# Scaling and shifting the transposed tokens in one VectorE step, with the modulation's last products reordered, in a one-core backbone layer

## The chip, the cores and the metric

The kernel runs on one NeuronCore of one Trainium2 chip. A time is the device time of one execution in microseconds. The trace is that of one profiled execution of the kernel before; its span runs from the first to the last instruction.

## The reference

One layer: a token-mixing block (windowed attention beside an mLSTM) and a SwiGLU block, each between norms, for 1024 latent tokens and 256 context tokens of width 1024, all in float32. What the change touches is the entrance of the layer, and one place where the mixing block's output projection meets the next norm:

```python
mod_x = (silu_c @ w_ada[layer] + b_ada[layer])[:, None, :]
mod_c = silu_cc @ w_ada[layer] + b_ada[layer]
sh_m, sc_m, gt_m, sh_f, sc_f, gt_f = jnp.split(mod_x, 6, axis=-1)
...
px = modulate(rms_norm(x, g_pre_mix[layer]), sh_m, sc_m) @ w_in[layer]
pc = modulate(rms_norm(ctx, g_pre_mix[layer]), csh_m, csc_m) @ w_in[layer]
...
mix_x = jnp.concatenate([att_x, ml_x], axis=-1) @ w_out[layer]
x = x + gt_m * rms_norm(mix_x, g_post_mix[layer])
```

with `modulate(h, shift, scale) = h * (1 + scale) + shift`.

## The kernel before

Every product that matters is taken in parts: `split` writes a value's rounded high half with a ScalarE cast and the rest, its low half, with a VectorE subtraction (L61, L62). `mm3` (L73 to L75) then issues three matmuls: high by high, high by low, low by high, on TensorE (PE in the profile).

**Modulation (L283 to L361).** For the sections scale (`sec` 1) and then shift (`sec` 0), eight 512 KB blocks `wa` of the weights arrive by DMA one after another. Five of a section's blocks are split into scratch space in `hh` and `hl`, and PE takes one pair of matmuls with the high half and one with the low half; three blocks (the table `PLAIN`) go through PE as plain float32. The sums `pr` have 4 rows; they are copied to SBUF (the first half by ScalarE, L344, the second by VectorE, L345), transposed into `pcol`, and combined into the per-channel columns `scol` (scale) and `hcol` (shift, L361). In section 0 the split of block 3 takes its low half on GpSimd (L302), and block 3's and block 6's low products are issued late. The first weights `w1` of the layer are split meanwhile, by `w1_split` (L274, L279).

**Token preparation (L184 to L256).** There are ten tiles of 128 tokens, 0 to 7 latent and 8 and 9 context. For each: load and sum of squares (`prep_a`, L190), scaling of the tokens (`xt`, L197, on GpSimd for most), eight transposes on PE into two PSUM halves `pt` (`prep_t`, L209), then per half a multiplication by `scol` on VectorE (`prep_m`, L223), an addition of `hcol` (`prep_b`, L236; on VectorE for tiles 0 and 1, on GpSimd from tile 2 on), a cast to `hh` (ScalarE, L251; for the first half of tile 0 L248 does all from PSUM) and the low half `hl` (VectorE, L252). `pt` has two buffers (tag `tp`) for tiles 1 to 9, so that a half can be transposed only when the half two before it has been read.

**First projections (L364 to L454).** `s1(i)` multiplies tile i by `w1`: 24 matmuls of 128x272 in two groups of 12, the first needing the first halves of `hh` and `hl`, the second the second halves (for tile 0 all `hh` products come first, L381, then the `hl` products, L384). Its sums go to the gate table `G` (VectorE, L398 and L400), to `av` (ScalarE L61 and VectorE L62) and to `V` (ScalarE, L403). `s2(i)` does the same with the second weights `w2`, whose halves are made by L450 and L451 in the turns of tiles 1 and 2; three tiles of `s2` are put between the `s1` from turn 3 on.

**What sets the order here.** From the start of the kernel to the end of these projections the order on each engine is chosen by a scheduler that works with its own table of costs; `tc.keep_in_program_order` pins single instructions to the written order. Each engine then works through its queue strictly in that order.

**Output projection (L1304 to L1336).** Here the written order holds (`tc.manual_schedule`). In turn n, `omm` multiplies row tile n, `opost1` and `opost2` form the norm, the residual and the next norm of tile n-1 (squares L1183 and L1191, scaling L1193), `otr` transposes its result on PE (L1205), `omod` modulates it (L1214), and `mixsplit(n, hf)` (L1170) splits one half of the mixing output of tile n into `mh` and `ml` for `omm`.

Of the kernel before, what the change touches and what calls it, by code (L numbers as in the profile page):

```python
# [9 lines left out]
F32 = mybir.dt.float32  # L10
F32R = mybir.dt.float32r
AF = mybir.ActivationFunctionType
# [4 lines left out]
P = 128  # L17
# [23 lines left out]
def body(tc, x, ctx, vecs, bcv, bada, gqm, gqf, wada, ws1, ws2, wt, wout, wfi, wfo,  # L41
# [156 lines left out]

    pts = {}

    def prep_t(i, keep=False):

        xt = xts.pop(i)
        pts[i] = []
        for b in range(2):
            pt = pa.tile([P, 4, P], F32, name="pt", tag="tp" if i else "mm", bufs=2 if i else 4)
            for k in range(4):
                kk = 4 * b + k
                t = pe.transpose(pt[:, k, :], xt[:, kk * P:(kk + 1) * P], ident)  # L209
                if keep and not kk:  # L210
                    tc.keep_in_program_order(t)
            pts[i].append(pt)

    raw2 = {}

    def prep_m(i):

        if i not in pts:
            prep_t(i)
        rw = hraw.pop(i)  # L220
        raw2[i] = [rw[:, 4 * b:4 * b + 4] for b in range(2)]
        for b in range(2):
            r = dve.tensor_tensor(raw2[i][b], pts[i][b], hcast(scol[:, i // NT, 4 * b:4 * b + 4]), MUL)  # L223
            if i == 1:
                tc.keep_in_program_order(r)

    def prep_b(i):

        if i not in raw2:
            prep_m(i)  # L230
# [3 lines left out]
        raws_ = raw2.pop(i)  # L234
        for b in (1, 0) if i == 0 else range(2):
            r = (dve if i < 2 else pool).tensor_tensor(raws_[b], raws_[b], hcast(hcol[:, q, 4 * b:4 * b + 4]), ADD)  # L236
            if i < 2:
                tc.keep_in_program_order(r)
            if i == 0 and b:
                w1_split(1, (1,))  # L240
        if i == 0:
            r2 = st[:, 12:13]
            tc.keep_in_program_order(dve.reciprocal(r2, r2))
        for b in range(2):
            h_ = hs[b][:, :, tok]
            if i + b == 0:
                for k in range(4):
                    act.activation(h_[:, k], pts[i][b][:, k], AF.Identity, scale=scol[:, q, k:k + 1],  # L248
                                   bias=hcol[:, q, k:k + 1])
            else:  # L250
                tc.keep_in_program_order(act.copy(h_, raws_[b]))  # L251
            r = dve.tensor_tensor(ls[b][:, :, tok], raws_[b], h_.bitcast(F32), SUB)  # L252
            if i == 0:
                tc.keep_in_program_order(r)
        if i == 0:
            prep_a2(2)  # L256
# [26 lines left out]
    PLAIN = {1: (0, 2, 4), 0: (0, 2, 7)}  # L283
    last, nsp, late = None, 0, []

    wm = pa.tile([P, 4, P], F32, name="warm", tag="tp", bufs=2)
    for i in range(11):
        pe.matmul(wm[:, i % 4], ones, ones, start=True, stop=True)
    for sec in (1, 0):
        pr = [pa.tile([4, 512], F32, name=f"pr{sec}{i}", tag="mm", bufs=4) for i in range(2)]  # L290
        for kt in range(KT):
            w = R(8 + kt, f"wa{sec}_{kt}", (D,))
            with tc.issue_after(last) if last is not None else ExitStack():
                last = dma(w, wada[kt * P:(kt + 1) * P, sec * D:(sec + 1) * D]).ins
            if kt in PLAIN[sec]:
                ops = ((cz4, w),)
            else:
                wh, wl = (t[1 - nsp // 4 % 2][:, nsp % 4] for t in (hh, hl))
                nsp += 1
                if (sec, kt) == (0, 3):  # L300
                    act.copy(wh, w)
                    pool.tensor_tensor(wl, w, wh.bitcast(F32), SUB)  # L302
# [5 lines left out]
            if (sec, kt) == (0, 3):  # L308
                low3 = ops.pop()
            if (sec, kt) == (0, 4):  # L310
                ops.insert(1, low3)
            if (sec, kt) == (0, KT - 2):
                late = ops[1:]
                ops = ops[:1]
            if (sec, kt) == (0, KT - 1):
                ops += late
            for n, (k, a, b) in enumerate(ops):
                for i in range(2):
                    r = pe.matmul(pr[i], a[:, k, :], b[:, i * 512:(i + 1) * 512], start=kt == 0 and n == 0,
                                  stop=kt == KT - 1 and n == len(ops) - 1)  # L320
                    if late:
                        tc.keep_in_program_order(r)
            if (sec, kt) == (0, 1):
                for i in range(2):
                    with tc.issue_after(last):
                        prep_a(i)
                        last = xd[i].ins
            if (sec, kt) == (0, 2):
                prep_t(0, True)
            if (sec, kt) == (0, 7):  # L330
                for i in range(2):
                    with tc.issue_after(last):
# [11 lines left out]
        act.copy(r4[:, 0:512], pr[0])  # L344
# [1619 lines left out]
```

## Time and profile before

| what | value |
|---|---|
| three runs | 1199.36, 1200.81, 1200.82 us; median 1200.81 us |
| profiled execution, its own time | 1200.47 us |
| its span | 1198.7 us (1.8 us lie around it) |
| PE busy | 1177.0 us, 98% of the span |
| VectorE (DVE) busy | 816.3 us |
| ScalarE (ACT) busy | 575.0 us |
| GpSimd (POOL) busy | 155.7 us |
| PE idle in the span | 21.7 us |

In the profile L12 is line 12 of the kernel before. Times of a timeline row are its start and its duration in us; a bracket behind a row is the idle time of its engine just before it and what ended that. The view of stretches gives, for each stretch, its length, the busy time (and the number of instructions) of PE, PE's weight loads, DVE, ACT and POOL, then the clock granted to PE as a share of full speed, the DMA share and GB/s. Rows of matmuls overlap: one starts before the modelled end of the one ahead.

### The profile page before, as it was taken

The numbers are of one execution on the slowest core, as the hardware profiler recorded it, in microseconds if no ns is written. First come the engines' busy times: TensorE is split into PE (matmuls) and PEld (weight loads), VectorE is DVE, ScalarE is ACT, GpSimd is POOL, SyncE is SP. The second block draws the span as 40 slices with busy tenths as digits, with TensorE's granted clock in tenths as the row PEclk, the third lists the DMA queues.
The fourth block names the chain that finished last, engine by engine and source line by source line (L and its number), as shares of the span: only waits on it lengthen the run. The fifth ranks groups of instructions, "written<-read, shape, count | busy, mean of one in ns | idle before, by whom it ended". The sixth has DMA issues, their size and how long they took to land.

```text
span 1198.7 us, 16356 instructions
## 1 busy us (share of the span) xinstructions
PE 1177.0 (98%) x5881; PEld 967.4 (81%) x5881; DVE 816.3 (68%) x1435; ACT 575.0 (48%) x1067; POOL 155.7 (13%) x197
## 2 busy tenths in 40 slices
PE   8899999999999999999999999999999999999997
PEld 3799888877878788788788888888888888888886
DVE  5863768853888795458877678676777656544567
ACT  5743442222777795687534333333333335434443
POOL 1550001215444461000000000000000000000000
PEclk9999999999999999999999999999999999999999
DMA  9522955557679971421133565656554557665853
GB/s 364 194 71 60 370 194 172 180 156 227 176 217 240 315 234 53 178 87 71 62 123 132 202 220 206 208 218 237 202 167 124 201 176 259 203 215 187 304 189 127
DMA packets 104616, 225.37 MB, mean 188 GB/s; under 512 B 10068, under 2 KB 39380, under 8 KB 103128
## 3 DMA queue, kind: packets, MB, share of 16 engines
q1 hardware_dynamic: 104536, 224.34, 56.3%
q8 instruction: 46, 0.75, 0.3%
q14 instruction: 34, 0.28, 0.1%
HBM read 162.43 MB, written 61.21 MB: 187 GB/s over the span
## 4 chain that ended last, share of the span: by engine, by line
PE 68%; DVE 4%; ACT 2%; issue 1%; DMA 0%; SPq 0%; POOL 0%; DVEq 0%; ACTq 0%
PE xv L75 8%; PE xv L73 8%; PE xv L74 8%; PE pt L75 6%; PE pt L74 6%; PE pt L73 6%; PE op L75 2%; PE op L73 2%; PE op L74 2%; PE fx L73 2%; PE fx L75 2%; PE fx L74 2%; PE pt L871 1%; PE pt L867 1%; PE pt L985 1%; PE fy L73 1%
## 5 line engine op out<-in xcount | busy, mean ns | idle before, releaser
L62 DVE TENSOR_TENSOR fo<-fr,fo 128x1024 fp32r<-128x1024 f32 x77 | 92.7, 1222 | 71.1 <-ACT fo L61 69.6
L61 ACT CAST fo<-fr 128x1024 fp32r<-128x1024 f32 x77 | 79.6, 1051 | 74.0 <-PE pt L75 36.5
L598 PE MATMUL t<-hh,th 128*128 128x512 f32 x208 | 82.4, 396 | 0.0
L599 PE MATMUL t<-hl,th 128*128 128x512 f32 x208 | 81.7, 393 | 0.0
L1380 ACT CAST wS<-wr 128x512 fp32r<-128x512 f32 x88 | 54.2, 622 | 56.1 <-PE pt L75 37.4
L1382 DVE TENSOR_TENSOR wS<-wr,wS 128x512 fp32r<-128x512 f32 x88 | 60.4, 689 | 20.7 <-ACT wS L1380 20.7
L73 PE MATMUL xv<-tT,wS 128*128 128x512 f32 x168 | 66.0, 393 | 0.0
L601 PE MATMUL t<-hh,tl 128*128 128x512 f32 x208 | 65.9, 394 | 0.0
L75 PE MATMUL xv<-tT,wS 128*128 128x512 f32 x168 | 65.6, 391 | 0.0
L74 PE MATMUL xv<-tT,wS 128*128 128x512 f32 x168 | 65.5, 390 | 0.0
L75 PE MATMUL op<-woh,ml 128*128 128x512 f32 x128 | 50.1, 392 | 1.5 <-DVE ml L62 1.5
L73 PE MATMUL op<-woh,mh 128*128 128x512 f32 x128 | 51.0, 398 | 0.0
L74 PE MATMUL op<-wol,mh 128*128 128x512 f32 x128 | 50.0, 390 | 0.0
L1131 DVE TENSOR_TENSOR wr<-wr 128x512 f32<-128x512 f32 x66 | 45.5, 690 | 1.4
L1414 ACT ACTIVATE es<-es 128x512 f32<-128x512 f32 x22 | 13.9, 632 | 66.5 <-DVE es L1134 66.5
L598 PEld LDWEIGHTS t<-hh,th 128*128 128x128 f32 x208 | 39.1, 188 | 8.2 <-issue 0.3
L599 PEld LDWEIGHTS t<-hl,th 128*128 128x128 f32 x208 | 39.1, 188 | 7.7 <-issue 0.7
L601 PEld LDWEIGHTS t<-hh,tl 128*128 128x128 f32 x208 | 37.4, 188 | 7.6 <-issue 1.4
L955 PE MATMUL s<-k,qh 128*128 128x256 f32 (+1 forms) x128 | 41.1, 331 | 2.0 <-ACT so L775 0.9
L73 PE MATMUL pt<-fo 128*128 128x512 f32 x110 | 42.8, 389 | 0.0
L75 PE MATMUL pt<-fo 128*128 128x512 f32 x110 | 42.8, 389 | 0.0
L74 PE MATMUL pt<-fo 128*128 128x512 f32 x110 | 42.8, 389 | 0.0
(1006 smaller groups left out, 3408.7 us busy)
## 6 DMA issues: line engine op xcount, KB each, us to landing
wr<-in_wfi SPq DMA_DIRECT2D x44, 512.0 KB, 4.6
wb<-in_wada SPq DMA_DIRECT2D x24, 512.0 KB, 6.0
s_d<-a SPq DMA_DIRECT2D x22, 512.0 KB, 6.9
bt<-in_wfo SPq DMA_DIRECT2D x44, 256.0 KB, 3.8
tb_d<-bt SPq DMA_DIRECT2D x11, 1024.0 KB, 3.9
fr<-s_d SPq DMA_DIRECT2D x44, 256.0 KB, 4.4
fr<-tb_d SPq DMA_DIRECT2D x44, 256.0 KB, 4.3
fr<-a_d SPq DMA_DIRECT2D x33, 256.0 KB, 4.5
```

What stands on the lines that cost most here:

```text
L61: act.copy(hi, raw)
L62: dve.tensor_tensor(lo, raw, hi.bitcast(F32), SUB)
L73: pe.matmul(ps, a[0], b[0], start=first, stop=False, **kw)
L74: pe.matmul(ps, a[0], b[1], start=False, stop=False, **kw)
L75: pe.matmul(ps, a[1], b[0], start=False, stop=last, **kw)
L598: pe.matmul(o, wh[:, kt], m[0], start=f, stop=False)
L599: pe.matmul(o, wh[:, kt], m[1], start=False, stop=False)
L601: pe.matmul(o, wl[:, kt], m[0], start=False, stop=l)
L955: pe.matmul(o, qh[:, h, :], k2[g][:, kc], start=True, stop=False)
L1131: dve.tensor_tensor(out, a, b, SUB)
L1380: act.copy(w[:, 0], raw)
L1382: dve.tensor_tensor(w[:, 1], raw, w[:, 0].bitcast(F32), SUB)
```

## The change

Four edits, of which three concern the first 80 us.

1. *Scaling and shifting in one step.* `prep_m` is gone. `prep_raw` reads each `pt` half from PSUM in four VectorE instructions of 128x128, each multiplying by one column of `scol` and adding one column of `hcol` (L219 of the new kernel, `tensor_scalar` with two per-partition operands). It stands in for one multiplication and one addition of 128x512. GpSimd keeps only the scaling of `xt`. Because the step needs `hcol`, nothing of it runs ahead of the shift columns any more; before, the multiplications of tiles 0 and 1 did.
2. *The modulation's last products.* Block 3 of section 0 is split like the others, its low half on VectorE. The products of blocks 3 to 7 are collected and issued in a fixed order: high 3, high 4, low 3, high 5, low 4, [first half of tile 1's transposes], high 6, low 5, plain 7, low 6, [second half of those transposes]. The copy of the first half of `pr` is pinned behind the casts of `w1`.
3. *Buffers.* The warm-up tile moves from tag `tp` to tag `mm`.
4. *Output projection.* In turn 2 alone, `mixsplit(2, 0)` is written ahead of `opost1(1)` instead of behind it.

```diff
-                if keep and not kk:
+                if keep:
                     tc.keep_in_program_order(t)
...
-        for b in range(2):
-            r = dve.tensor_tensor(raw2[i][b], pts[i][b], hcast(scol[:, i // NT, 4 * b:4 * b + 4]), MUL)
-            if i == 1:
-                tc.keep_in_program_order(r)
...
+    def prep_raw(i, b):
+
+        q = i // NT
+        raw = hraw[i][:, 4 * b:4 * b + 4]
+        for k in range(4):
+            kk = 4 * b + k
+            r = dve.tensor_scalar(raw[:, k], pts[i, b][:, k], scol[:, q, kk:kk + 1], hcol[:, q, kk:kk + 1], MUL, ADD)
+            if i < 2:
+                tc.keep_in_program_order(r)
+        return raw
...
-        for b in (1, 0) if i == 0 else range(2):
-            r = (dve if i < 2 else pool).tensor_tensor(raws_[b], raws_[b], hcast(hcol[:, q, 4 * b:4 * b + 4]), ADD)
...
+            if b not in raws_:
+                raws_[b] = prep_raw(i, b)
...
-    wm = pa.tile([P, 4, P], F32, name="warm", tag="tp", bufs=2)
+    wm = pa.tile([P, 4, P], F32, name="warm", tag="mm", bufs=4)
...
-                if (sec, kt) == (0, 3):
-                    act.copy(wh, w)
-                    pool.tensor_tensor(wl, w, wh.bitcast(F32), SUB)
-                else:
-                    split(wh, wl, w)
+                split(wh, wl, w)
...
+            if (sec, kt) > (0, 2) and not sec:
+                late += ops
+                ops = ()
             if (sec, kt) == (0, KT - 1):
-                ops += late
+
+                ops = late = [late[k] for k in (0, 2, 1, 4, 3, 6, 5, 8, 7)]
             for n, (k, a, b) in enumerate(ops):
+                if late and n == 5:
+                    prep_t(1, True, (0,))
...
-            if (sec, kt) == (0, 6):
-                prep_t(1, True)
-                prep_m(0)
-                prep_m(1)
+        if sec == 0:
+            prep_t(1, True, (1,))
...
-        act.copy(r4[:, 0:512], pr[0])
+        r = act.copy(r4[:, 0:512], pr[0])
+        if sec == 0:
+            tc.keep_in_program_order(r)
...
+        if n == 2:
+            mixsplit(n, 0)
         opost1(n - 1)
-        mixsplit(n, 0)
+        if n != 2:
+            mixsplit(n, 0)
```

On VectorE, just behind the low halves of tile 0, the kernel before had these rows (`hraw_234` is tile 1, `hraw_319` tile 2; `hh_101`, `hl_103` are first halves, `hh_102`, `hl_104` second halves):

```order
L236 TENSOR_TENSOR hraw_234<-hraw_234,hcol 128x512 x2
L398 TENSOR_TENSOR G<-slab,bcr 128x2x4
L400 TENSOR_TENSOR G<-slab,bcr 128x2x4
L223 TENSOR_TENSOR hraw_319<-pt,scol 128x512
L252 TENSOR_TENSOR hl_103<-hraw_234,hh_101 128x4x128
L223 TENSOR_TENSOR hraw_319<-pt,scol 128x512
L252 TENSOR_TENSOR hl_104<-hraw_234,hh_102 128x4x128
L62 TENSOR_TENSOR av_91<-slab,av_91 128x128
L435 RECIPROCAL st<-st 128x1
L252 TENSOR_TENSOR hl_103<-hraw_319,hh_101 128x4x128
```

In the new kernel the same place on VectorE reads so (`hraw_234` is tile 1, `hraw_315` tile 2):

```order
L219 TENSOR_SCALAR hraw_234<-pt,scol,hcol 128x128 x4
L247 TENSOR_TENSOR hl_103<-hraw_234,hh_101 128x4x128
L219 TENSOR_SCALAR hraw_234<-pt,scol,hcol 128x128 x4
L387 TENSOR_TENSOR G<-slab,bcr 128x2x4
L389 TENSOR_TENSOR G<-slab,bcr 128x2x4
L219 TENSOR_SCALAR hraw_315<-pt,scol,hcol 128x128 x5
L247 TENSOR_TENSOR hl_104<-hraw_234,hh_102 128x4x128
L219 TENSOR_SCALAR hraw_315<-pt,scol,hcol 128x128 x3
L62 TENSOR_TENSOR av_91<-slab,av_91 128x128
```

Tile 1's second low half now stands behind five of the eight steps of tile 2, and the remaining three stand ahead of `av`.

Further on, on VectorE behind the preparation of tile 2, the kernel before had (`w2l_477` is the low half of the second weights, `hraw_366` tile 4; tile 3's multiplications were ahead of this place):

```order
L451 TENSOR_TENSOR w2l_477<-wr_0_478,w2h_476 128x768
L398 TENSOR_TENSOR G<-slab,bcr 128x2x4
L400 TENSOR_TENSOR G<-slab,bcr 128x2x4
L223 TENSOR_TENSOR hraw_366<-pt,scol 128x512
L451 TENSOR_TENSOR w2l_477<-wr_2_482,w2h_476 128x768
```

The new kernel has there (`w2l_493` the same weights, `hraw_368` tile 3):

```order
L440 TENSOR_TENSOR w2l_493<-wr_0_494,w2h_492 128x768
L387 TENSOR_TENSOR G<-slab,bcr 128x2x4
L389 TENSOR_TENSOR G<-slab,bcr 128x2x4
L440 TENSOR_TENSOR w2l_493<-wr_2_498,w2h_492 128x768
L219 TENSOR_SCALAR hraw_368<-pt,scol,hcol 128x128 x8
```

All eight steps of tile 3 stand behind both weight rows and behind the gate rows of tile 2; on PE, tile 3's transposes stand behind all of `s1(2)`, and tile 4's first half directly behind them.

In the output projection, ScalarE had in turn 2 (`t_5211` is tile 1's norm, `mh` the half of tile 2 in question):

```order
L1214 ACTIVATE mix<-pt,hfc,sfc 128x128 x8
L1183 ACTIVATE t_5211,st<-op 128x1024
L178 ACTIVATE st<-st,epst 128x1
L61 CAST mh<-mix 128x512
L61 CAST b11h<-mix 128x4x128
L1191 ACTIVATE t_5211,st<-xt_5113 128x1024
```

and has now (`t_5255` is tile 1's norm):

```order
L1203 ACTIVATE mix<-pt,hfc,sfc 128x128 x8
L61 CAST mh<-mix 128x512
L1172 ACTIVATE t_5255,st<-op 128x1024
L178 ACTIVATE st<-st,epst 128x1
L61 CAST b11h<-mix 128x4x128
L1180 ACTIVATE t_5255,st<-xt_5153 128x1024
```

The cast of `mh` moved from behind the first square of tile 1's norm to ahead of it.

More of the change, by code (lines that the diff above doesn't have):

```diff
@@ L199, in body, with prep_t @@
     pts = {}
-    def prep_t(i, keep=False):
-        xt = xts.pop(i)
-        pts[i] = []
-        for b in range(2):
+    def prep_t(i, keep=False, parts=(0, 1)):
+        xt = xts[i]
+        for b in parts:
             pt = pa.tile([P, 4, P], F32, name="pt", tag="tp" if i else "mm", bufs=2 if i else 4)
@@ L209, in prep_t, with prep_b @@
                 t = pe.transpose(pt[:, k, :], xt[:, kk * P:(kk + 1) * P], ident)
-                if keep and not kk:
+                if keep:
                     tc.keep_in_program_order(t)
[L212 to L218, printed above, removed]
-            prep_t(i)
[L220 to L223, printed above, removed]
-            if i == 1:
-                tc.keep_in_program_order(r)
-    def prep_b(i):
-        if i not in raw2:
-            prep_m(i)
+            pts[i, b] = pt
+    def prep_raw(i, b):
[7 more added lines that the diff above has]
+        return raw
+    def prep_b(i):
+        if (i, 1) not in pts:
+            prep_t(i)
         q, j = (0, i) if i < NT else (1, i - NT)
@@ L233, in prep_b @@
         tok = slice(j * P, (j + 1) * P)
-        raws_ = raw2.pop(i)
-        for b in (1, 0) if i == 0 else range(2):
[L236 to L240, printed above, removed]
+        raws_ = {}
         if i == 0:
+            raws_[1] = prep_raw(0, 1)
+            w1_split(1, (1,))
             r2 = st[:, 12:13]
@@ L245, in prep_b @@
             h_ = hs[b][:, :, tok]
+            if b not in raws_:
+                raws_[b] = prep_raw(i, b)
             if i + b == 0:
                 for k in range(4):
-                    act.activation(h_[:, k], pts[i][b][:, k], AF.Identity, scale=scol[:, q, k:k + 1],
-                                   bias=hcol[:, q, k:k + 1])
+                    act.activation(h_[:, k], pts[0, 0][:, k], AF.Identity, scale=scol[:, 0, k:k + 1],
+                                   bias=hcol[:, 0, k:k + 1])
             else:
```

7 lines of the change are left out of this document (removed).

## The prediction

> **What bounds the kernel now.** I read the page's busy times first, then stretches of the span, then PE's waits, then the timeline where PE waits. The page's first part:
>
> ```profile
> PE 1177.0 (98%) x5881; PEld 967.4 (81%) x5881; DVE 816.3 (68%) x1435; ACT 575.0 (48%) x1067; POOL 155.7 (13%) x197
> ```
>
> TensorE is busy in all but 21.7 us. The change does not alter its matmuls, so it can only move PE's idle time and its clock. Stretches of 3.4 us around the token preparation, and the long one behind:
>
> ```profile
> 33.72:37.13 3.41, 2.27 (x16) 1.83 (x16) 3.34 (x10) 3.36 (x9) 0.11 (x1) 1.00 0.97 379
> 37.13:40.54 3.41, 3.41 (x16) 3.37 (x16) 2.62 (x6) 2.45 (x4) 0.00 (x0) 0.50 0.09 36
> 40.54:43.95 3.41, 2.72 (x22) 2.50 (x22) 2.76 (x6) 2.35 (x6) 1.70 (x2) 1.00 0.26 58
> 43.95:47.36 3.41, 3.24 (x27) 3.02 (x26) 2.63 (x8) 2.90 (x8) 2.64 (x3) 1.00 0.24 96
> 47.36:50.78 3.42, 3.42 (x30) 3.34 (x28) 2.42 (x6) 1.94 (x5) 3.42 (x4) 1.00 0.51 156
> 50.78:54.20 3.42, 2.00 (x15) 1.84 (x14) 3.42 (x7) 2.49 (x7) 3.42 (x3) 1.00 0.65 187
> 54.20:280.00 225.80, 225.80 (x1292) 194.72 (x1291) 153.93 (x296) 78.80 (x131) 51.07 (x61) 1.00 0.53 173
> ```
>
> Behind 54.2 us PE has no gap up to 280, so what is won or lost ahead of it moves the end by as much. From 40.54 to 54.2 PE is idle for 0.69 + 0.17 + 0 + 1.42 = 2.28 us. From 37.13 to 40.54 it is granted half its clock. VectorE has little room: it is idle 0 to 1 us per stretch and full in the last of them. PE's two longest waits that the change aims at:
>
> ```profile
> PE op L75 <- DVE ml L62: 1.5, 1, 1.5
> PE pt L209 <- POOL xt L197: 1.4, 1, 1.4
> ```
>
> **The modulation's end.** Timeline rows of this place:
>
> ```profile
> 18.68 1.23 DVE L62 TENSOR_TENSOR hl<-wa,hh 128x1024 fp32r<-128x1024 f32 x1 [1.54 <-ACT hh L61]
> 23.85 2.39 POOL L302 TENSOR_TENSOR hl<-wa,hh 128x1024 fp32r<-128x1024 f32 x1
> 25.08 2.25 DVE L62 TENSOR_TENSOR hl<-wa,hh 128x1024 fp32r<-128x1024 f32 x1 [0.42 <-ACT hh L61]
> 26.61 1.05 ACT L61 CAST hh<-wa 128x1024 fp32r<-128x1024 f32 x1 [0.23 <-DMA wa<-in_wada]
> 30.57 1.19 ACT L274 CAST w1h<-wr 128x544 fp32r<-128x544 f32 x2 [0.17 <-DMA wr<-in_ws]
> 31.00 1.88 PE L319 MATMUL pr<-wa,cz 128*4 128x512 f32 x4
> 32.81 0.62 PE L319 MATMUL pr<-hl,cs 128*4 128x512 f32 x2
> 33.24 0.57 ACT L344 COPY Vc<-pr 4x512 f32<-4x512 f32 x1 [1.48 <-PE pr L319]
> 35.25 0.68 DVE L236 TENSOR_TENSOR hraw<-hraw,hcol 128x512 f32<-128x512 f32 x1
> ```
>
> Block 6's cast ends at 26.61 + 1.05 = 27.66. With block 3 on VectorE (1.23 instead of GpSimd's 2.39, and no 2.25 beside it) and the multiplications gone from this place, the last low half ends at about 28.9; on PE the plain block then runs from 28.8 to 30.7 and the last pair to 31.3, where it ended at 33.4. But that gain of 2.1 is cut: the copy of `pr` stands behind the casts of `w1`, which end at 30.57 + 1.19 = 31.76 and which a DMA holds. The copy starts 33.24 - 31.76 = **1.5 us earlier**, and so do the shift columns: VectorE is free of them at 35.25 - 1.5 = 33.8.
>
> **Token preparation.** Here lies the cost, and I follow VectorE's new queue. Durations:
>
> ```profile
> 37.30 1.29 DVE L252 TENSOR_TENSOR hl<-hraw,hh 128x512 fp32r<-128x512 f32 x2
> 556.99 1.37 DVE L1212 TENSOR_SCALAR mix<-pt,sfc,hfc 128x128 f32<-128x128 f32 x4 [0.43 <-PE pt L1205]
> 66.08 0.22 DVE L441 TENSOR_SCALAR mF<-cst 128x128 f32<-128x128 f32 x1
> L223 DVE TENSOR_TENSOR hraw<-pt,scol x20: 675/680/694, 24.0 to 78.8; 128x512 f32<-128x512 f32 x20
> L252 DVE TENSOR_TENSOR hl<-hraw,hh x16: 666/808/1484, 37.3 to 72.4; 128x512 fp32r<-128x512 f32 x16
> L236 POOL TENSOR_TENSOR hraw<-hraw,hcol 128x512 f32<-128x512 f32 x16 | 20.8, 1318 | 9.9 <-DVE hraw L223 9.9
> L451 DVE TENSOR_TENSOR w2l<-wr,w2h x4: 1122/1270/1791, 50.0 to 59.7; 128x768 fp32r<-128x768 f32 x4
> L251 ACT CAST hh<-hraw x15: 602/620/632, 36.5 to 71.7; 128x512 fp32r<-128x512 f32 x15
> 44.09 0.28 DVE L62 TENSOR_TENSOR av<-slab,av 128x128 fp32r<-128x128 f32 x1
> 44.40 0.27 ACT L403 COPY V<-slab 128x128 f32<-128x128 f32 x1 [1.50 <-DVE av L62]
> 39.15 1.80 PE L384 MATMUL slab<-w1h,hl 128*128 128x272 f32 x8
> 66.36 0.29 PE L73 MATMUL slab<-w1h,hh 128*128 128x272 f32 x1
> 66.73 0.29 PE L73 MATMUL slab<-w1h,hh 128*128 128x272 f32 x1
> 70.33 1.04 PE L209 MATMUL pt<-vec,xt 128*128 128x128 f32 x8
> 71.12 0.37 PE L73 MATMUL slab<-w1h,hh 128*128 128x272 f32 x1
> ```
>
> The new step has the form of L1212 (PSUM in, two per-partition operands): 1.37 us for four, against 0.68 for the multiplication it replaces. It could cost as little as four of L441 (0.22, from SBUF), 0.9 at most, or four unoverlapped L1212, 1.6; I take 1.35, the same form. For tiles 2 to 9 that is 16 x (1.35 - 0.68) = 10.7 us more of VectorE, and 20.8 us less of GpSimd. Some comes back: `hl` took 0.67 to 1.48 us, and it is the long ones that had GpSimd at work beside them, while L223, which reads one operand from PSUM, stayed at 0.68 throughout. At 0.67 instead of the median 0.81, 16 x 0.14 = 2.2 us return.
>
> So VectorE gets some 8.5 us more to do in a stage where it had little room. What counts is where PE waits for it. PE's measures: three 128x272 matmuls in 0.37 (0.125 each), eight transposes in 71.12 - 70.33 = 0.8. Reckoned times, with a handover of 0.05 each:
>
> - Tile 0: two additions of 0.68 become two groups of 1.35, so its first `hl`, at 37.30 before, starts at 37.30 - 1.5 + 1.3 = 37.1 and ends at 37.8. PE's `hh` products end at 36.9. **Wait 0.9**; `s1(0)` ends at 39.0.
> - Tile 2's first transposes need the `pt` half that tile 1's first group reads until 39.8. **Wait 0.8**. Cast of 0.62 and low half of 0.68 follow: PE goes on at 41.2, having had 0.65 of work. **Wait 0.7**. The other ten matmuls end at 42.5.
> - Tile 1's second half: its group ends at 42.4, the cast at 43.1. Its low half stands behind the gate rows and five steps of tile 2 (5 x 0.34 = 1.7) and ends at 45.0. PE had transposes (0.4) and two matmuls. **Wait 1.7**; `s1(1)` ends at 46.3.
> - Tile 2: ScalarE's cast stands behind the copy of `V`, which waits for `av`, which stands behind three steps: 45.0 + 1.0 + 0.28 + 0.27 + 0.62 = 47.2. **Wait 0.9**, then the low half, **0.5**; `s1(2)` ends at 50.7.
> - Tile 3: behind `s1(2)` come the gate rows (0.2), the second weight row (about 1.0, below the 1.12 that it took beside GpSimd) and the first group (1.35), to 53.3; PE has 0.8 of tile 3's transposes and then needs this half free for tile 4. **Wait 1.8**.
>
> Sum 7.3 us, against 2.28 before: **+5.0**. From there on PE has `s2(0)` to do between the halves, and by the same reckoning VectorE stays ahead.
>
> The clock: the half-rate stretch follows on one in which PE had little but the tiny `pcol` transposes. In it eight matmuls took 1.80 instead of 1.0; sixteen such cost 1.6 us. In the new order PE's idle time lies in other places; at 50.8 to 54.2 it works only some 1.2 of 3.4 us, before it worked 2.0 there and kept its clock. I count half a stretch, 0.8: **-0.8**.
>
> **The cast in turn 2.** Rows of both engines:
>
> ```profile
> 489.47 1.07 ACT L1183 ACTIVATE t<-op 128x1024 f32<-128x1024 f32 x1
> 490.86 0.60 ACT L61 CAST mh<-mix 128x512 fp32r<-128x512 f32 x1
> 493.89 1.06 ACT L1191 ACTIVATE t<-xt 128x1024 f32<-128x1024 f32 x1 [1.90 <-DVE xt L1134]
> 494.51 0.50 PE L75 MATMUL op<-woh,ml 128*128 128x512 f32 x1 [1.47 <-DVE ml L62]
> 495.60 1.15 ACT L1193 ACTIVATE t<-xt,st 128x1024 f32<-128x1024 f32 x1 [0.23 <-DVE st L179]
> 496.92 1.03 PE L1205 MATMUL pt<-vec,t 128*128 128x128 f32 x8
> ```
>
> The wait of 1.47 goes: `ml` is ready by 491. But PE's next work, the transposes L1205 of tile 1's norm, starts at 496.92, and L1193, which they read, ends at 495.60 + 1.15 = 496.75: a slack of 0.17. PE would arrive at 495.45 and wait for that chain; and the chain, which begins at L1183 without a gap, starts later by the cast put ahead of it (0.6, overlapping to about 0.5). Its old place cost nothing there (ScalarE waited 1.90 behind it). So -1.47 + 1.47 + 0.5 less the slack: **+0.4**, between 0 and 0.6.
>
> The buffer move costs nothing: the warm-up tile is done before the shift section needs its slot.
>
> **Sum** against the profiled execution: -1.5 + 5.0 - 0.8 + 0.4 = +3.1, 1200.47 + 3.1 = **1203.6 us**. The median of the runs, 1200.81, is 0.3 above the profiled one; I stay with 1203.6. What a measurement of this kernel tells from no change is about 0.2%, 2.4 us, so this is just slower.
>
> **Rivals.**
>
> *VectorE keeps up (faster).* If four steps cost 0.9, as from L441, each of the six groups on PE's path is 0.45 shorter and the waits come to 7.3 - 2.7 = 4.6; with no half-rate stretch (-1.6) that is -1.5 + 2.3 - 1.6 + 0.4 = -0.4. It is faster by over 2.4 us only if PE's waits from 34 to 54 us stay below 2.3 - 2.4 + 1.5 + 1.6 - 0.4 = 2.6 us, which asks in addition that tile 1's low half and tile 3's group not hold PE; with the waits at 1.5 the time is 1197. For it: the 1.4 us behind GpSimd goes, and 2.2 us of contention. Against it: the rows of L1212, which read PSUM as the new step does, where L441 reads SBUF. Chance 0.16. The Trainium skill's page "VectorE: DVE Perf Modes", section "Why PSUM operands drop a tier", says that a float32 instruction with a PSUM operand runs at one element per cycle, where one from SBUF can run at two; by that rule the price of L441 is not to be had here, and the two rows agree with it.
>
> *It cancels (same).* The scheduler has put PE work between the halves, and handovers may be shorter than reckoned; with 4.5 to 5 us of waits instead of 7.3, and no half-rate stretch or one, the time is 1200 to 1202. A form of it is that the cast does win its 1.5 us because tile 1's chain has slack that the trace hides: 1201.7. Chance 0.32.
>
> *The clock falls more often (slower still).* Three stretches in the new order (37 to 40.5, 44 to 47.4, 50.8 to 54.2) have PE at work under half of the time. Each half-rate stretch behind them costs up to 1.6 us; two give 1203.6 + 2.4 = 1206.0. For it: the stretch ahead of the half-rate one had sixteen matmuls, half of them the tiny transposes. Against it: some of the loss hides in waits for VectorE. Chance 0.17. The Trainium skill's page "TensorE: Matmul & The Clock Gate", section "What's actually happening", says that a window of about 3.4 us with little activity halves the clock until a busy one has passed; the half-rate stretch of this trace is one such length, and that rule speaks against a change that spreads PE's gaps.
>
> *The forecast itself:* chance 0.35, 1202.5 to 1205.
>
> **The numbers.** Slower by over 0.2%: 0.35 + 0.17 = 0.52; same 0.32; faster 0.16. The range from 1198.6 to 1207.2 leaves out about one in ten at each end: below, the rival with all waits gone; above, three half-rate stretches or the unoverlapped step at 1.6.
>
> **What would show it.** In the new profile: the copy of `pr` at 31.8; four steps in 1.35; `hl` near 0.67; PE waiting for `hl` or for `pt` between 37 and 54 for some 7 us, longest ahead of tile 1's second half and of tile 4's transposes; no wait at `ml` in turn 2, but one of 1.5 to 2 us at L1205's line right behind. I am wrong if PE's waits ahead of 54 us are under 4 us, or if those transposes start without a wait.

## The result and the profile after

The changed kernel takes 1208.26 us (median of 4 runs, 1207.25 to 1208.95), the kernel before 1200.82 (4 runs, 1199.36 to 1202.66). The ratio is 1.0060, 95% interval 1.0048 to 1.0072: slower by 7.2 us. I had forecast 1203.6, 3.1 us slower, and a range up to 1207.2, which the measured time exceeds. The sign was right; the forecast was less than half of what came. The profiled execution took 1207.25 us, 6.8 more than the profiled one of before.

Busy times of the kernel after. TensorE has the same 5881 matmuls and as much busy time as before; VectorE has 6 us more (I had reckoned 8.5), GpSimd 25 us less:

```profile
PE 1177.4 (98%) x5881; PEld 968.3 (80%) x5881; DVE 822.2 (68%) x1492; ACT 574.0 (48%) x1067; POOL 130.5 (11%) x180
```

The same stretches as before the change (columns PE, PEld, DVE, ACT, POOL busy, then the granted clock, DMA share and GB/s):

```profile
33.72:37.13 3.41, 0.46 (x8) 0.38 (x7) 2.84 (x12) 1.10 (x3) 0.11 (x1) 0.75 0.97 381
37.13:40.54 3.41, 1.89 (x8) 1.89 (x9) 1.84 (x6) 2.40 (x6) 0.00 (x0) 0.50 0.11 41
40.54:43.95 3.41, 3.41 (x24) 3.41 (x23) 2.73 (x8) 1.27 (x2) 0.00 (x0) 0.75 0.00 0
43.95:47.36 3.41, 2.28 (x20) 2.06 (x18) 3.41 (x12) 2.43 (x6) 0.00 (x0) 1.00 0.05 11
47.36:50.78 3.42, 2.35 (x15) 1.92 (x16) 2.94 (x10) 3.27 (x9) 2.10 (x2) 1.00 0.40 145
50.78:54.20 3.42, 3.42 (x30) 3.27 (x28) 2.40 (x7) 3.26 (x10) 2.20 (x2) 1.00 0.00 0
54.20:280.00 225.80, 223.96 (x1285) 193.36 (x1286) 159.69 (x338) 79.66 (x135) 31.64 (x43) 1.00 0.54 175
```

The large hole is at the very start, 33.7 to 39 us, where I had expected 0.9 us of waiting. TensorE's waits:

```profile
PE slab L370 <- ACT hh L243: 4.5, 1, 4.5
PE pt L1194 <- ACT t L1182: 1.9, 1, 1.9
PE pt L208 <- DVE hraw L219: 1.8, 1, 1.8
PE pcol L341 <- ACT Vc L331: 1.8, 1, 1.8
PE slab L75 <- DVE hl L247: 1.7, 2, 1.1
...
PE slab L73 <- ACT hh L246: 0.5, 1, 0.5
```

The second and third are forecast waits (1.5 to 2 and 1.8). The fourth, for the copy of `pr`, was 0.4 before: TensorE is done with the products earlier, but the copy comes only 0.3 earlier. The first is in no step of mine. Its place in the timeline, ScalarE, VectorE and TensorE in order of time:

```profile
31.81 1.19 ACT L269 CAST w1h<-wr 128x544 fp32r<-128x544 f32 x2 [1.36 <-DMA wr<-in_ws]
32.91 0.57 ACT L331 COPY Vc<-pr 4x512 f32<-4x512 f32 x1
34.69 0.17 DVE L350 TENSOR_TENSOR hcol<-pcol,hcol 128x8 f32<-128x8 f32 x1
34.77 1.36 DVE L219 TENSOR_SCALAR hraw<-pt,scol,hcol 128x128 f32<-128x128 f32 x4
36.75 1.35 DVE L219 TENSOR_SCALAR hraw<-pt,scol,hcol 128x128 f32<-128x128 f32 x4
38.14 1.50 ACT L243 ACTIVATE hh<-pt,hcol,scol 128x128 fp32r<-128x128 f32 x4 [3.28 <-DVE hraw L219]
38.65 0.59 PE L370 MATMUL slab<-w1h,hh 128*128 128x272 f32 x1 [4.46 <-ACT hh L243]
39.67 1.29 DVE L247 TENSOR_TENSOR hl<-hraw,hh 128x512 fp32r<-128x512 f32 x2 [1.57 <-ACT hh L243]
```

ScalarE's activations of tile 0's first half read `pt`, `scol` and `hcol`. All three are there at 34.86, yet they start at 38.14, right behind VectorE's second group of four steps, which reads the same `pt` half. TensorE begins tile 0 at 38.65, 3.0 later than before.

How late is TensorE at the end of the stage? Its last products of context with the second weights start here (before, then after; the last number before the semicolon):

```profile
L73 PE MATMUL slab<-w2h,ch x16: 334/334/340, 113.7 to 122.0; 128*128 128x384 f32 x16
```

```profile
L73 PE MATMUL slab<-w2h,ch x16: 334/334/340, 118.7 to 126.9; 128*128 128x384 f32 x16
```

So 4.9 us were lost ahead of this point, where my steps had 2.7 (-1.5 + 5.0 - 0.8). The rest lies in turn 2 of the output projection. The timeline of that place after the change, and stretches of the start and of this place, cut where the clock changes:

```profile
502.03 1.09 PE L1194 MATMUL pt<-vec,t 128*128 128x128 f32 x8 [1.95 <-ACT t L1182]
502.88 0.65 PE L73 MATMUL op<-woh,mh 128*128 128x512 f32 x1
503.32 0.63 PE L74 MATMUL op<-wol,mh 128*128 128x512 f32 x1
```

```profile
32.01:35.42 3.41, 0.65 (x8) 0.57 (x8) 1.88 (x9) 2.81 (x6) 0.11 (x1) 1.00 1.03 402
35.42:38.83 3.41, 0.18 (x1) 0.18 (x2) 2.68 (x9) 0.69 (x2) 0.00 (x0) 0.50 0.56 217
38.83:42.24 3.41, 3.41 (x16) 3.41 (x17) 2.57 (x6) 2.37 (x5) 0.00 (x0) 0.50 0.01 4
499.63:503.04 3.41, 1.46 (x11) 1.04 (x11) 0.75 (x3) 3.15 (x7) 0.00 (x0) 1.00 0.51 163
503.04:506.45 3.41, 3.41 (x10) 2.64 (x9) 0.77 (x2) 2.76 (x8) 0.00 (x0) 0.50 0.44 144
```

The wait of 1.47 for `ml` went and one of 1.95 came, 0.5 us more, as forecast. But behind it TensorE is granted half its clock for 3.41 us: matmuls that follow each other at 0.23 us elsewhere come at 0.44 (502.88, 503.32), which costs another 1.7 us. 4.9 + 0.5 + 1.7 = 7.1, against the 6.8 measured in these two executions. The profiled execution, at 1207.25 us, is the fastest of the four: two others, 1208.67 and 1208.95, were granted 0.992 of the clock on average, where it was granted 0.995.

### The profile page after: what moved, and what is told of

Read it like the earlier page. It is cut to its first block, busy times and chain, and to the rows that moved or that the text cites. A ratio compares the mean times of both kernels' runs of the same rounds, so it can differ in the third digit from the quotient of the medians.

```text
span 1205.4 us, 16396 instructions
## 1 busy us (share of the span) xinstructions
PE 1177.4 (98%) x5881; PEld 968.3 (80%) x5881; DVE 822.2 (68%) x1492; ACT 574.0 (48%) x1067; POOL 130.5 (11%) x180
## 4 chain that ended last, share of the span: by engine, by line
PE 80%; DVE 7%; DMA 5%; ACT 3%; issue 3%; POOL 1%; SPq 1%; DVEq 0%; ACTq 0%; POOLq 0%
PE xv L75 8%; PE xv L73 8%; PE xv L74 8%; PE pt L73 6%; PE pt L75 6%; PE pt L74 6%; PE op L74 2%; PE op L73 2%; PE op L75 2%; PE slab L74 2%; PE slab L73 2%; PE slab L75 2%; PE fx L73 2%; PE fx L75 2%; PE fx L74 2%
```

## The experiments

Twelve kernels, each timed beside the kernel before on its chip; a ratio is to that kernel, with its 95% interval, and differences in us are those of the ratios (the 4.8 and 7.7 us in some expectations are differences of medians). By these intervals, how far two kernels of this series differ is known to about 2 us. The scheduler can answer an edit with other orders elsewhere: in the traces, experiments 2, 4 and 10 leave the other engines' order up to 90 us as it was, and 12 that of 11. In all the others it differs from 40 to 45 us on also where the edit asks for nothing, and their numbers hold both. Theory A at the outset: the start of tile 0 is what I missed. Its rival: VectorE's longer queue for the other tiles is the cost. For each profile I also give TensorE's time at the last product of context above, less what half-rate stretches cost ahead of it (busy time x (1 - granted clock)), as *clock-free front*: before 122.0 - 1.7 = 120.3, after 126.9 - 1.8 = 125.1.

**1. Activations written first.**

```diff
         for b in range(2):
             h_ = hs[b][:, :, tok]
-            if b not in raws_:
-                raws_[b] = prep_raw(i, b)
             if i + b == 0:
...
-            else:
+            if b not in raws_:
+                raws_[b] = prep_raw(i, b)
+            if i + b:
```

> The changed kernel, with ScalarE's four activations of tile 0's first half written ahead of VectorE's four steps on the same PSUM half (in the changed kernel they stand behind them). Theory A (the two readers of one PSUM half are taken one after the other, in the order in which they are written, and that is what the start lost): the activations start near 34.9 instead of 38.1, TensorE's wait of 4.5 us for them falls under 1.5 us; VectorE's four steps now wait for ScalarE, until about 36.5 to 36.8, so that a wait of about 2 us for the first low half appears. Net -2 us, and up to -3.7 us if a half-rate stretch goes too: 1204.5 to 1206.3. Theory B (VectorE's longer queue is what costs): VectorE has the same instructions as before the edit, so nothing changes, 1208.

Timeline of this kernel:

```profile
34.01 1.49 ACT L241 ACTIVATE hh<-pt,hcol,scol 128x128 fp32r<-128x128 f32 x4
34.50 0.60 PE L370 MATMUL slab<-w1h,hh 128*128 128x272 f32 x1 [1.07 <-ACT hh L241]
36.00 1.35 DVE L219 TENSOR_SCALAR hraw<-pt,scol,hcol 128x128 f32<-128x128 f32 x4
```

The activations start with the end of `hcol` and TensorE's wait falls from 4.46 to 1.07. Up to there only the order of the two readers of one PSUM half was changed, so the cause of the hole is shown. (VectorE's group, which now stands second, starts at 36.00, behind the activations' end at 35.50; VectorE was busy until then, so whether it would have waited is not shown.) The time gained nothing that can be told from the noise and is above the 1204.5 to 1206.3 expected: 1207.14 (1204.71 to 1208.95), ratio 1.0057 (1.0044 to 1.0071). The clock-free front is 126.0 - 4.5 = 121.5, 3.6 better than after, but this execution paid 4.5 us for half-rate stretches there, 2.7 more. The longest waits that are left:

```profile
51.06 1.09 PE L208 MATMUL pt<-vec,xt 128*128 128x128 f32 x8 [1.27 <-POOL xt L425]
54.01 1.12 PE L208 MATMUL pt<-vec,xt 128*128 128x128 f32 x4 [1.86 <-DVE hraw L219]
```

**2. The cast of turn 2 put back.** `mixsplit(n, 0)` stands behind `opost1(n - 1)` in every turn.

> The changed kernel, with the cast of turn 2 back behind tile 1's norm. Theory A (the moved cast costs an extra half-rate stretch: in the changed kernel nine matmuls behind the wait of 1.95 us follow each other at 0.43 us instead of 0.23): the wait of 1.5 us for the low half returns, the wait of 1.9 us at the transposes goes, and no half-rate stretch is seen there: -2.1 us, 1206.2. Theory B (as I reckoned it, a swap of waits): -0.4 us, 1207.9. Theory C (the moved cast gains its 1.5 us): +1.5 us, 1209.8.

1206.72 (1204.46 to 1207.91), ratio 1.0047 (1.0034 to 1.0060): 1.6 us back of the 7.2. The wait for `ml` is there again at 1.5 us, and no stretch near it is at half rate. That is nearest to theory A (1206.2); theory B (1207.9) lies at the edge of the interval.

**3. Tile 0 in two steps again.**

```diff
         raw = hraw[i][:, 4 * b:4 * b + 4]
+        if i == 0:
+            tc.keep_in_program_order(dve.tensor_tensor(raw, raw, hcast(hcol[:, 0, 4 * b:4 * b + 4]), ADD))
+            return raw
...
+            if (sec, kt) == (0, 6):
+                for b in range(2):
+                    dve.tensor_tensor(hraw[0][:, 4 * b:4 * b + 4], pts[0, b], hcast(scol[:, 0, 4 * b:4 * b + 4]), MUL)
```

> The changed kernel, with tile 0 alone scaled and shifted in two steps again: its multiplications early, two additions of 128x512 behind the shift columns. All other tiles keep the one step. Theory A (the start of tile 0 is the cost): ScalarE's activations start near 34.9, TensorE's wait ahead of the first products falls from 4.5 to about 1 us, the low halves follow without a wait: -3.5 us, and to -5.2 us if the second half-rate stretch goes: 1203 to 1204.8. Theory B (the extra work on VectorE for tiles 1 to 9 is the cost): little changes, above 1206.5.

1205.29 (1203.68 to 1206.26), ratio 1.0036 (1.0023 to 1.0048): 2.9 us back, a little less than the 3.5 expected without the clock. TensorE waits for tile 0's activations for 1.1 us instead of 4.5; the clock-free front is 125.4 - 3.4 = 122.0. The waits at 45 to 55 us stay (1.20 for a cast, 1.86 for `pt`).

**4. The cast alone, on the kernel before.**

```diff
+        if n == 2:
+            mixsplit(n, 0)
         opost1(n - 1)
-        mixsplit(n, 0)
+        if n != 2:
+            mixsplit(n, 0)
```

> The kernel before the change, with only the cast of turn 2 moved ahead. Theory A (wait of 1.9 us at the transposes and a half-rate stretch behind it): +2.1 us on the kernel before, 1202.9. Theory B (waits swapped, no clock): +0.4 us, 1201.2. Theory C (gains the wait of 1.5 us): 1199.3.

1201.57 (11 runs, 1199.27 to 1203.21), ratio 1.0007 (0.9998 to 1.0016): +0.8, between theories A and B; C is out. Its profile shows why it can be either. The wait at the transposes is 1.9 us, but this execution was granted its full clock behind it, and also at 37 us, where the first profile had the half rate:

```profile
490.24:493.65 3.41, 3.41 (x17) 2.75 (x15) 3.21 (x4) 1.06 (x2) 0.00 (x0) 1.00 0.00 0
493.65:497.06 3.41, 1.46 (x11) 1.13 (x10) 0.82 (x3) 3.15 (x7) 0.00 (x0) 1.00 0.42 160
497.06:500.48 3.42, 3.42 (x16) 2.82 (x15) 0.64 (x2) 3.30 (x9) 0.00 (x0) 1.00 0.40 147
```

(These stretches are cut at the wait. On the grid of half-rate stretches described in the last section, the wait of this execution falls into two lengths, 491.43 to 494.84 and 494.84 to 498.26, in which TensorE worked for 2.53 and 2.35 us.) Six profiles have this wait of 1.9 us in turn 2; in four of them the half rate follows, and in none of the eight that have the wait of 1.5 us in its place. An estimate of the price is then 0.5 + 4/6 x 1.7 = 1.6, the figure of experiment 2 and within the interval of this one, -0.2 to 1.9.

**5. One step for tiles 2 to 9 alone, on the kernel before.**

```diff
+            if i > 1:
+                for k in range(4):
+                    kk = 4 * b + k
+                    dve.tensor_scalar(raw2[i][b][:, k], pts[i][b][:, k], scol[:, i // NT, kk:kk + 1],
+                                      hcol[:, i // NT, kk:kk + 1], MUL, ADD)
+                continue
...
-            r = (dve if i < 2 else pool).tensor_tensor(raws_[b], raws_[b], hcast(hcol[:, q, 4 * b:4 * b + 4]), ADD)
-            if i < 2:
+            if i < 2:
+                r = dve.tensor_tensor(raws_[b], raws_[b], hcast(hcol[:, q, 4 * b:4 * b + 4]), ADD)
```

> The kernel before the change, with the one step (four VectorE instructions of 128x128 from PSUM) for tiles 2 to 9 alone; tiles 0 and 1, the modulation and turn 2 stay as before. Theory A (only tile 0's start costs): as the kernel before, 1200.7, or up to 1 us more. Theory B (VectorE's extra work behind the start costs on its own): TensorE waits for VectorE's steps at 50 to 56 us, some 2 us of new waits in all, and in about half of the executions a half-rate stretch of 1.7 us behind them: 1203 to 1204.

1205.37 (1203.16 to 1206.94), ratio 1.0036 (1.0023 to 1.0049): +4.3 with nothing of tile 0 or turn 2 touched. Theory B, and above its figure: the rival to my first theory holds as well. TensorE waits for the step's hold on the PSUM half and for low halves:

```profile
PE pt L209 <- DVE hraw L226: 2.3, 1, 2.3
PE slab L75 <- DVE hl L258: 1.9, 3, 0.8
```

The clock-free front is 124.4 - 1.6 = 122.8, 2.5 later than before. The other 1.8 fits the clock: the wait of 2.3 us, until 52.5, runs into a half-rate stretch in the profile, where the kernel before has none. The granted clock of each execution is on record; it averages 0.9962 over these five and 0.9979 over the twenty of the kernel before on that chip, and 0.0017 x 1201 = 2.0 us.

**6. After, without the one step for tiles 2 to 9.** Tiles 0 and 1 keep it.

```diff
+        if i > 1:
+            dve.tensor_tensor(raw, pts[i, b], hcast(scol[:, q, 4 * b:4 * b + 4]), MUL)
+            pool.tensor_tensor(raw, raw, hcast(hcol[:, q, 4 * b:4 * b + 4]), ADD)
+            return raw
```

> The changed kernel, with tiles 2 to 9 in two steps again (multiplication on VectorE, addition on GpSimd); tiles 0 and 1 keep the one step, and the modulation and turn 2 stay changed. Theory A (the one step of tiles 2 to 9 is the larger cost: alone on the kernel before it cost 4.8 us): the waits for VectorE at 45 to 56 us go, 1204 to 1205.5, and what is left of the 7.7 us is tile 0's start and turn 2. Theory B (tile 0's late start is the larger one, and behind it VectorE's extra work hides): 1206.5 to 1208.

1204.73 (1203.90 to 1205.95), ratio 1.0034 (1.0022 to 1.0047): 3.1 us back, as theory A has it. The clock-free front is 125.4 - 2.1 = 123.3. The wait of 1.8 us for the `pt` half is gone, but one of 1.8 for `xt` from GpSimd has come (1.4 in the kernel before). The wait of 4.5 at the start and both clock losses (about 40 and 501 us) are still there. Of the three parts undone one by one, tile 0 gives 2.9, tiles 2 to 9 give 3.1 and the cast 1.6; their sum is 7.6, against 7.2 lost. Each of the three is known only to about 2 us, so the sum is no proof of the shares.

**7. The modulation's part alone.** All tiles in two steps, tile 0's multiplications early, turn 2 as before; the products' order, block 3 on VectorE, the pinned copy and the warm-up tile as after.

> The kernel before the change, with the modulation's part of it alone: last products in the new order, low half of block 3 on VectorE, copy of the first half of pr pinned behind the casts of w1, warm-up tile moved. All tiles are scaled and shifted in two steps, tile 0's multiplications early, tile 1's in its turn, tiles 2 to 9 with GpSimd's additions; turn 2 as before. Theory A (the gain is cut by the casts of w1, whose second block lands late): shift columns 0.5 us earlier, 1200.2. Theory B (the full 1.5 us of my reckoning, where the block lands in time): 1199.2. Theory C (it costs, as tile 1's multiplications come later): 1201.5 or more.

1201.09 (11 runs, 1200.47 to 1202.09), ratio 1.0003 (0.9994 to 1.0012): no gain that can be measured. ScalarE and VectorE there:

```profile
31.52 1.19 ACT L271 CAST w1h<-wr 128x544 fp32r<-128x544 f32 x2 [1.65 <-DMA wr<-in_ws]
32.62 0.57 ACT L336 COPY Vc<-pr 4x512 f32<-4x512 f32 x1
33.94 0.17 DVE L355 TENSOR_TENSOR hcol<-pcol,vec 128x8 f32<-128x8 f32 x1 [1.01 <-PE pcol L346]
```

TensorE is done with the products at 31.3, as reckoned, but the block of `w1` lands at 31.5, a microsecond later than in the profile before, and the copy behind its casts with it. The clock-free front is 123.1 - 1.7 = 121.4, 1.1 later than before, and yet this profiled execution took the same 1200.47 us: the kernel before has a wait of TensorE of 0.9 us for `so` (L775) at 295 us, which is not found here, nor in the changed kernel. So what is lost ahead of the front isn't always lost at the end; the prediction took for granted that it is.

**8. That copy ahead of those casts, and a little work for TensorE.** As 7, and: `act.copy(r4[:, 0:512], pr[0])` ahead of `w1_split(1, (-1,))`, four transposes of the identity ahead of the shift columns' transposes and six behind.

> As the modulation's part alone, with two things more: the copy of the first half of pr stands ahead of the casts of the second block of w1 instead of behind them, and four transposes of the identity stand ahead of the shift columns' transposes and six behind them, read by nobody. Theory A (the casts, which a DMA holds, are what keeps the shift columns late, and a little TensorE work there keeps its clock): shift columns at about 33.3 instead of 34.7, a half-rate stretch in few executions: 1198.5. Theory B (the casts of w1 then come late, and TensorE or VectorE wait for them instead): 1200.7.

1203.24 (10 runs, 1201.53 to 1206.04), ratio 1.0024 (1.0014 to 1.0033): a miss. The copy starts at 31.12, tile 0's products at 34.43 (before 35.61), and no half-rate stretch is in the profile; but the front, 124.3 with no clock to take off, is 4.0 late. A lead of 1.2 us at the start was lost behind it: TensorE waits for casts (1.9 us in two waits), for a low half (1.3), for `xt` (1.1) and for a `pt` half (1.3). Both edits, and the order that the scheduler made of them, are in this number; which of them holds those tiles I didn't separate.

**9. Work in TensorE's holes after the change.**

```diff
         if sec == 0:
             prep_t(1, True, (1,))
+            wf = pa.tile([P, 4, P], F32, name="fill", tag="gx", bufs=2)
+            for k in range(12):
+                tc.keep_in_program_order(pe.transpose(wf[:, k % 4], ident, ident))
...
+        for k in range(0 if sec else 30):
+            tc.keep_in_program_order(pe.transpose(wf[:, k % 4], ident, ident))
```

> The changed kernel, with 12 transposes of the identity into an unused PSUM tile ahead of the shift columns' transposes and 30 behind them, so that TensorE works (about 0.11 us each) through most of its two waits of 1.8 and 4.5 us. Nothing reads them. Theory A (TensorE's clock falls to half for 3.4 us behind a stretch of the same length in which it worked less than about half): no half-rate stretch between 35 and 42, the products of tile 0's high halves follow at full rate; the changed kernel loses 1.7 us there in every execution, so 1206.6. Theory B (the clock there has another cause, or the fillers delay the shift columns by as much): no gain, 1208.3 or more.

1207.50 (1205.95 to 1209.32), ratio 1.0056 (1.0044 to 1.0069): 0.5 us, not 1.7, and not to be told from no gain. The clock does what theory A says, at the place:

```profile
34.41:37.82 3.41, 2.63 (x25) 2.39 (x22) 3.12 (x10) 0.25 (x1) 0.00 (x0) 1.00 0.78 303
37.82:41.23 3.41, 3.15 (x20) 2.79 (x21) 2.12 (x5) 2.81 (x6) 0.00 (x0) 1.00 0.02 7
```

Tile 0's products end 1.6 earlier than after. But TensorE then waits 1.6 us for low halves, 1.3 for `xt` from GpSimd and 1.9 for the `pt` half, and runs at half rate from 54 to 61 us. The clock-free front, 128.7 - 2.7 = 126.0, is no better than after the change (125.1). In experiments 8 and 9 TensorE was made faster at the start and waited later. Experiment 1 is different: its front kept all of the 3.4 us by which the wait at the start fell, and in its profile 2.7 us of that went to the clock.

**10. Eight transposes of the identity in the kernel before,** between the shift columns' transposes and tile 0's products. No other engine's order changes.

> The kernel before the change, with eight transposes of the identity into an unused PSUM tile between the shift columns' transposes and tile 0's first products (nobody reads them; VectorE's, ScalarE's and GpSimd's instructions are the same and in the same order). TensorE works through most of its wait of 1.0 us there. Theory A (a stretch of 3.4 us in which TensorE works under about half halves its clock in the next): the half-rate stretch at 37 to 40.5 us, which most executions of the kernel before should have, goes in most of them: -1.0 to -1.7 us, 1199. Theory B (the clock there has another cause, or the eight run into the products): no change, 1200.6, or up to 0.5 us more.

```profile
33.72:37.13 3.41, 3.07 (x24) 2.66 (x24) 3.34 (x9) 3.38 (x9) 0.11 (x1) 1.00 0.95 375
37.13:40.54 3.41, 3.41 (x28) 3.20 (x27) 3.35 (x9) 2.44 (x4) 0.00 (x0) 1.00 0.05 18
```

1199.90 (11 runs, 1198.83 to 1201.77), ratio 0.9991 (0.9982 to 1.0000): 1.1 us faster than the kernel before, at the edge of what can be told, and the fastest of all. The stretch that ran at half rate has the full clock.

**11. One step for tiles 2 to 9, their low halves on GpSimd.** Experiment 5, and `(dve if i < 2 else pool).tensor_tensor(ls[b][:, :, tok], ...)`.

> The kernel before the change, with the one step for tiles 2 to 9 (which alone gave 1205.4), and now the low halves of these tiles on GpSimd in place of VectorE. VectorE has then per half 1.35 us (four steps) where the kernel before has 0.68 + 0.81 us, so no more than before, while each PSUM half is still held for 1.35 us by the step. Theory A (VectorE's load is what the one step costs): most of the 4.8 us comes back, 1201 to 1202.5. Theory B (the longer hold of the PSUM half, and not the load, is the cost): 1203.5 or more. Theory C (GpSimd's low halves, at 1.3 us, are late instead): 1203.5 or more too, but with TensorE waiting for GpSimd's low halves and not for the PSUM halves.

1202.77 (11 runs, 1202.10 to 1204.33), ratio 1.0013 (1.0004 to 1.0023): 2.8 of the 4.3 us come back, nearest to theory A. What is left is the hold of the PSUM half, and a little of theory C:

```profile
PE pt L209 <- DVE hraw L226: 1.6, 1, 1.6
...
PE slab L75 <- DVE hl L258: 1.5, 2, 0.7
...
PE slab L75 <- POOL hl L258: 1.1, 1, 1.1
```

The clock-free front is 124.0 - 1.7 = 122.3, only 0.5 better than in experiment 5. The rest of the gain fits the clock: behind the shorter wait at 52 us this profile keeps it, and the granted clock averages 0.9978 over these eleven executions, where the kernel before has 0.9976 on that chip; in experiment 5 it was 0.0017 below.

**12. Experiments 10 and 11 together.**

> The kernel before with the one step for tiles 2 to 9, their low halves on GpSimd, and the eight transposes of the identity behind the shift columns' transposes. It is both edits together: by theory A of each 1199.5 to 1201, by the rivals 1203.5 or more.

1202.04 (11 runs, 1201.65 to 1204.89), ratio 1.0012 (1.0003 to 1.0021): between what the two theories expect, and not faster than the kernel before. The one step for tiles 2 to 9 doesn't pay here even with VectorE relieved. Why the eight transposes, which gave 1.1 us in experiment 10, give 0.1 here is open.

## Why the prediction was wrong

- *Price of the four steps* (1.35 taken): right, 1.36 and 1.35. The rival in which VectorE keeps up is out.
- *Tile 0* ("PE's `hh` products end at 36.9. **Wait 0.9**"): this step failed. I let ScalarE's activations start with the shift columns, as they had before. In the new order VectorE's group on the same half is written ahead of them, so they wait for it: 4.5 us of TensorE's time instead of 0.9 for the low half. I had followed the queue of VectorE and not the new order of two engines at one tile. Before, VectorE's reader of that half, the multiplication, was done long ahead. Experiment 1 shows the cause; with tile 0 in two steps again (experiment 3) 2.9 us come back. The same order was in a row that I had read: the copy of `V` (44.40, idle for 1.50 until `av`) takes other columns of `slab` than `av` does and needs nothing of it, and still starts behind VectorE's read of that PSUM tile. I counted that wait for tile 2 and did not look for its like at tile 0.
- *The later waits of the token preparation* (0.8 + 0.7 + 1.7 + 0.9 + 0.5 + 1.8): right in kind, and the last to the tenth, but their sum was 4.0 and not 6.4. The first two didn't come: tile 0's products, late and at half rate, ended at 43.5, and by then VectorE had read tile 1's first half (42.2) and all but finished its low half (43.6). The others were 1.1, 0.5, 0.6 and 1.8. Alone, without the late start, the one step for tiles 2 to 9 costs 4.3 us, tile 0's part aside.
- *The modulation's end* (-1.5): this step failed too, by less. I had seen that a DMA holds the copy behind the casts of `w1`, and then took the landing time of one profile as given; in the new kernel the block landed 1.2 later and the shift columns came 0.5 earlier. Alone, with the order that the scheduler made of it, this part gained nothing that can be measured (experiment 7).
- *The clock* (half a stretch in place of one, -0.8): the term with the wrong sign. While TensorE has work, the profile after has three stretches at half rate, of which the first lies in the wait and costs nearly nothing; the two others cost 3.4 us, against 1.7 before. My rival with the more frequent half rate named the mechanism, but looked for it between 37 and 54 us, where the two later of its three places kept their clock, and not in turn 2.
- *The cast in turn 2* (+0.4): waits right (1.95 - 1.47 = 0.5). The half rate behind the longer wait was missing, and so the price: 1.6 us in experiment 2, 0.8 in experiment 4, neither clear of 0 by itself.

So the forecast had the later waits and the exchange of waits in turn 2 right in kind, and lacked two things: the order at tile 0's PSUM half and the half rate in turn 2. What stays open is how the 7.2 us divide among the parts to better than about 2 us each, and what made experiment 8 lose its lead.

## What to carry to other kernels

When an operation moves to another engine, list for each tile that it reads who else reads it, and in what order these are written now: a second reader can wait for the first though it needs nothing of it. A wait that grows from 1.5 to 1.9 us may cost more than 0.4: look at what the clock does behind it. And where TensorE waits for other engines all along a stage, a faster start can be handed back in the next waits, as in experiments 8 and 9: measure at the end of the stage, and not only at the wait that went.

## What the runs showed of the hardware

- The half-rate stretches lie on a fixed grid of 3.41 us whose offset to the kernel's start differs between executions: after the change they begin at 35.42, 38.83 and 503.04, and 503.04 - 35.42 is 137 such lengths; in the profile before one begins at 37.13, half a length off that grid. Whether a length is at half rate goes with TensorE's busy time in the length ahead. 1.46 us (499.63 above) was followed by half rate; in experiment 1 the same wait fell across the grid otherwise, and 1.67 was followed by the full rate, 1.09 by half:

```profile
497.54:500.95 3.41, 1.67 (x8) 1.05 (x6) 1.43 (x3) 2.45 (x4) 0.00 (x0) 1.00 0.38 154
500.95:504.36 3.41, 3.21 (x18) 2.81 (x19) 1.29 (x2) 3.41 (x10) 0.00 (x0) 1.00 0.50 154
50.40:53.81 3.41, 1.09 (x8) 0.86 (x8) 3.41 (x6) 1.67 (x5) 3.18 (x2) 1.00 0.26 45
53.81:57.22 3.41, 3.21 (x12) 3.21 (x13) 3.41 (x12) 2.79 (x5) 1.56 (x1) 0.50 0.90 336
```

  (The 2.27 us ahead of the half-rate stretch of the kernel before hold 0.75 us of 4x4 transposes, which seem to count for little.) In the fourteen profiles, each cut on its own grid up to 1185 us and without these transposes, 18 lengths at the full clock were followed by half rate: 15 with at most 1.54 us of work, the others with 1.63, 1.82 and 2.50. None of those followed by the full rate had less than 1.59. So a wait of 1.9 us costs its 1.7 us of clock or not by how it falls on the grid. That is one source of the 2 to 4 us by which times of one kernel differ: of the 62 executions of the kernel before that were timed beside the experiments, the 7 with a mean granted clock of 0.999 took 1199.8 us on average, the 37 with 0.998 1200.8, the 13 with 0.997 1201.6 and the 5 with 0.996 1203.1. The Trainium skill's page "TensorE: Matmul & The Clock Gate", section "What's actually happening", says that the window runs free of the kernel, which these rows bear out; it speaks of an idle window as what brings the half rate, and here one with 1.46 us of work was enough.
- Two engines' reads of one PSUM tile were taken one behind the other: ScalarE's activations stood 3.28 us until VectorE's four steps had read the half (after the change), and the copy of `V` 1.50 us until VectorE had read other columns of `slab` (before). In experiment 1, with the order turned round, the reads didn't overlap either, but VectorE was busy until its turn. The Trainium skill's page "PSUM — Partial Sum Buffer", section "PSUM bank collisions raise a hardware error", says that two engines must not touch one bank in the same partitions at once, reads included; no run here shows such a collision, only the order that keeps them apart.
- The low half of 128x512 on VectorE took 0.68 us (median of 16) with GpSimd's additions gone, and 0.81 before with them; the prediction had reckoned 0.67:

```profile
L247 DVE TENSOR_TENSOR hl<-hraw,hh x16: 669/676/1094, 39.7 to 80.7; 128x512 fp32r<-128x512 f32 x16
```
